# A fused pool and attention layer: three edits to the order of the work in the later projection slots

## The chip, the cores and the metric

The kernel runs on one core of a Trainium2 chip. A core has five engines that run their own instruction queues in order: TensorE (PE, matrix products; its weight loads are listed as PEld), VectorE (DVE), ScalarE (ACT), GpSimd (POOL) and SyncE (SP, which here issues the transfers). The metric is the device time of one execution, in microseconds (us), lower is better. The kernel before takes 346.24 us, the median of three runs (345.97 to 347.31).

## What is computed

One decoder layer over 1024 tokens of width 1024, in float32:

```
h = rmsnorm(x, norm_pre)
pool_u, pool_gate, q, k, v, attn_gate = split(h @ w_in)        # 512, 512, 512, 128, 128, 512 columns
pool  = (mean over the last 2/4/8/16 tokens of pool_u - pool_u) @ pool_w * pool_scale * silu(pool_gate)
attn  = sliding_window_attention(q, k, v, sinks) * silu(attn_gate)
y     = concat(pool, attn) @ w_out
out   = x + rmsnorm(y, norm_post)
```

## The kernel before

Every large product is made of float16 parts. A weight chunk of 1024 rows and 128 columns is bounded (`bound_w`, the sum of absolute values of each row, on ACT), the bound is spread over the partitions by a transpose on PE (`spread`, L82, one buffer `ps_sp`), `scale_w` takes a power of two from it on DVE (L87, L73 to L77, L213), `high_w` writes the high half on ACT (L219) and `low_w` the rest on DVE (L223). `proj` (L283) then makes three products for each of eight steps k: high by high, high by low, low by high; 24 products of 512 columns in all, into one of two accumulators (`ps_acc`).

The program's middle is a loop over slots `s` (L780). A slot is one chunk of columns for one half (512) of the tokens: slots 0 to 9 are k and q, 10 to 17 the pool gate, 18 to 25 `u` (the pool's input), 26 to 33 the attention's gate. The order within a slot is written out by hand, and each engine follows it in order. In the slots that matter here, 20 to 33, it is, in the kernel before:

- `pool_windows` (L482, on DVE): the window sums of the `u` part that landed in the slot before, one to four additions `win` (L489) and a subtraction `res` (L495).
- `low_w` of a chunk whose high half was made in the slot before, then the low parts of the output weights, `low_wo` (L563, on DVE), by a table (L802): one in each of slots 24 and 25, none in 26 and 27, two in each of 28 to 30 as far as their high parts exist, and so on.
- `proj`, with `middle` called ahead of step 4 of 8: there stand the `spread` and scale of the chunk that is due three slots later (in slots 23 to 26) or of a block of 128 tokens of the concatenation (`scale_cat`, in slots 31 to 33), `high_w`, and the pool's product `pool_mm` (L504, `mixed`) of the sums made one slot earlier.
- on ACT then `bound_w` or `bound_cat`, then `split_wo` (L560), the high part of one of the eight chunks of the output weights (slots 23 to 30), and then the slot's landing: `land_u` (L472, `ug`) or the gate's SiLU (`gt`, L529), which empties the accumulator.

After slot 33 comes the output loop (L861): for each block of 128 tokens two groups of 24 products `y`, which walk the output weights' chunks in the order 4, 5, 6, 7, 0, 1, 2, 3.

Of the kernel before, what the change touches and what calls it, by code (L numbers as in the profile page):

```python
# [22 lines left out]
KT = D // P  # L23
# [12 lines left out]
def trunk(ctx: ExitStack, tc, x, w_in, pool_w, pool_scale, attn_sinks, w_out, norm_pre, norm_post, out):  # L36
# [168 lines left out]
    halves = {}  # L205
# [15 lines left out]
    def low_w(ch):  # L221
        w, s = whl[ch], halves.pop(ch)
        nc.vector.scalar_tensor_tensor(  # L223
            w[:, 1], raws.pop(ch), s, w[:, 0], op0=ALU.mult, op1=ALU.subtract
        )
# [54 lines left out]
        split(pv, DOWN, vst[:, 0, tt, :], vst[:, 1, tt, :])  # L280


    def proj(ch, half, middle=None):  # L283
        w = whl[ch]
        acc = ps_acc.tile([P, 512], F32, tag="acc", name="acc")
        for k in range(KT):
            if k == 4 and middle:
                middle()
            for i, (a, b) in enumerate(PASSES):
                nc.tensor.matmul(  # L290
                    acc, w[:, a, k, :], hT[:, b, k, half_of(half)],
                    start=k == 0 and i == 0, stop=k == KT - 1 and i == 2,
                )
        return acc
# [172 lines left out]
    pool_in, pool_out, pool_acc = {}, {}, {}  # L467
# [175 lines left out]
    with tc.manual_schedule(engines={ENG.PE, ENG.Activation, ENG.DVE, ENG.Pool, ENG.SP}):  # L643

        nc.scalar.dma_start(pre, norm_pre[0:1, :])
        load_x(0)
        load_x(1)
        load_w(K)
        load_x(2)
        load_x(3)  # L650
        load_w(V)
        load_w(QS[0])
        load_w(QS[1])
        load_x(4)
        load_x(5)
        accs = {0: ps_acc.tile([P, 512], F32, tag="acc", name="acc")}

        def part(tt):
            products(accs[0][:, block_of(tt)], [
                (whl[K][:, a, k, :], hT[:, b, k, block_of(tt)]) for a, b in PASSES for k in range(KT)  # L660
            ])

        def unit(s):
            ch, half = slots[s]
            accs[s] = proj(ch, half)

        def land_unit(s):
            land_slot(*slots[s], accs.pop(s))

        gains()  # L670
        norm_scan(0)
        norm_scale(0)
        flip(0)
        norm_scan(1)
        norm_scale(1)
        bound_w(K)
        spread_w((K,))
        flip(1)
        norm_scan(2)
        scale_w((K,))  # L680
        norm_scale(2)
        norm_scan(3)
        land_hi(0)
        high_w(K)
        land_lo(0)
        norm_scale(3)
        flip(2)
        low_w(K)
        load_w(QS[2])
        load_x(6)  # L690
        land_hi(1)
        bound_w(V)
        spread_w((V,))
        land_lo(1)
        flip(3)
        scale_w((V,))
        land_hi(2)
        land_lo(2)
        land_hi(3)
        high_w(V)  # L700
        part(0)
        land_lo(3)
        low_w(V)
        load_w(QS[3])
        load_x(7)
        bound_w(QS[0])
        bound_w(QS[1])
        for tt in range(1, 4):
            part(tt)
        spread_w((QS[0], QS[1]))  # L710
        norm_scan(4)
        land_unit(0)
        scale_w((QS[0], QS[1]))
        high_w(QS[0])
        high_w(QS[1])
        norm_scale(4)
        low_w(QS[0])
        low_w(QS[1])
        load_constants()
        v_tile(0)  # L720
        v_tile(1)
        norm_scan(5)
        v_tile(2)
        v_tile(3)
        bound_w(QS[2])
        norm_scale(5)
        unit(1)
        bound_w(QS[3])
        norm_scan(6)
        spread_w((QS[2], QS[3]))  # L730
        flip(4)
        flip(5)
        norm_scan(7)
        norm_scale(6)
        land_hi(4)
        land_hi(5)
        scale_w((QS[2], QS[3]))
        land_lo(4)
        high_w(QS[2])
        high_w(QS[3])  # L740
        unit(2)
        land_lo(5)
        norm_scale(7)
        land_unit(1)
        low_w(QS[2])
        low_w(QS[3])
        flip(6)
        flip(7)
        land_hi(6)
        land_lo(6)  # L750
        unit(3)
        land_hi(7)
        land_lo(7)
        land_unit(2)
        v_tile(4)
        v_tile(5)
        constants()
        unit(4)
        land_unit(3)
        v_tile(6)  # L760
        v_tile(7)
        land_unit(4)
        scale_v()
        scale_qk()


        loads = iter(PGS + US + AGS)

        def load_next():
            ch = next(loads, None)  # L770
            if ch:
                load_w(ch)

        for _ in range(4):
            load_next()

        wo_hi = wo_lo = 0
        state = {"wo": False}
        last = len(slots)
        for s in range(5, last):  # L780
            ch, half = slots[s]
            n, odd = (s - 5) // 2, (s - 5) % 2
            if not odd:
                if 2 <= n <= NB + 1:
                    pv_land(n - 2)
                if 1 <= n <= NB:
                    mask(n - 1)
                if n < NB:
                    score_mm(n)
            elif n < NB:  # L790
                turn(n)
            if 20 <= s < 24:
                gate = cat[:, s - 20, :]
                nc.scalar.activation(gate, gate, AF.Silu)
            gates = list(pool_out)
            for key in list(pool_in):
                pool_windows(*key)

            for c2 in list(halves):
                low_w(c2)  # L800
                load_next()
            for _ in range((1, 1, 1, 0, 0, 2, 2, 2, 2, 2, 2)[s - 23] if s >= 23 else 0):  # L802
                if wo_lo < wo_hi:
                    low_wo(wo_lo)
                    wo_lo += 1


            def middle():
                for key in list(bounds):
                    if key[0] in ("wo", "c"):  # L810
                        spreads[key] = spread(bounds.pop(key))
                        if key[0] == "c":
                            scale_cat(key[1])
                        else:
                            pow2_of(widest(spreads.pop(key)), wop, wos, 14)
                            state["wo"] = True
                    elif first_slot[key] == s + 3:
                        spread_w((key,))
                        scale_w((key,))
                        high_w(key)  # L820
                if not odd and 1 <= n <= NB:
                    divide(n - 1)
                for key in gates:
                    pool_mm(*key)

            acc = proj(ch, half, middle)
            if odd and 1 <= n <= NB:
                pv_mm(n - 1)
            if odd and n < NB:
                turn_low(n)  # L830

            for c2 in order:
                if first_slot[c2] == s + 5:
                    bound_w(c2)

            if 9 <= s < 9 + KT:
                wo_raw["b", s - 9] = load_wo(s - 9)
            if 11 <= s < 11 + KT:
                bound_wo(s - 11)
            if s == 11 + KT:  # L840
                m = bounds["wo", 0] = col("wom")
                nc.vector.tensor_reduce(m, wom, axis=AX.X, op=ALU.max)
            if s >= 30:
                bound_cat(s - 30)
            if s >= 23 and wo_hi < KT:
                split_wo(wo_hi)
                wo_hi += 1
            if not odd and n < NB:
                score_land(n)
            for key in gates:  # L850
                pool_gate(*key)
            land_slot(ch, half, acc)
            if not odd and n < NB:
                exps(n)
            if s == 5 + 2 * NB + 1:
                open_late()
            if 21 <= s < 21 + KT:
                wo_raw["o", s - 21] = load_wo(s - 21)
            if s >= last - 2:
                load_res(s - last + 2)  # L860
        for n in range(NB):  # L861
            if n + 2 < NB:
                load_res(n + 2)
            if n + 4 < NB:
                bound_cat(n + 4)
            if n == NB - 1:
                out_last(n)
                break
            accs = []
            for nh in range(2):  # L870
                accs.append(out_mm(n, nh))
                for key in list(bounds)[:1]:
                    spreads[key] = spread(bounds.pop(key))
                    scale_cat(key[1])
            out_store(n, accs)
# [32 lines left out]
```

## Time and profile before

| | before |
|---|---|
| median of three runs | 346.24 us (345.97 to 347.31) |
| the profiled execution | 346.77 us |
| span of its instructions | 345.1 us, 1.67 us less |
| PE busy | 323.6 us, 94% of the span |
| DVE busy | 199.1 us, 58% |
| ACT busy | 168.9 us, 49% |
| POOL busy | 66.2 us, 19% |

The busy shares are averages over stages that have different limits. A row of the timeline has the start in us from the span's start, the time it took, the engine, line, operation, what is written and read, and in brackets the engine's idle time just before it and what ended that. The times of products overlap: a product that starts 0.216 us after another still shows 0.38 us.

### The profile page before, as it was taken

The numbers are of one execution on the slowest core, as the hardware profiler recorded it, in microseconds if no ns is written. First come the engines' busy times: TensorE is split into PE (matmuls) and PEld (weight loads), VectorE is DVE, ScalarE is ACT, GpSimd is POOL, SyncE is SP. The second block draws the span as 40 slices with busy tenths as digits, with TensorE's granted clock in tenths as the row PEclk, the third lists the DMA queues.
The fourth block names the chain that finished last, engine by engine and source line by source line (L and its number), as shares of the span: only waits on it lengthen the run. The fifth ranks groups of instructions, "written<-read, shape, count | busy, mean of one in ns | idle before, by whom it ended". The sixth has DMA issues, their size and how long they took to land.

```text
span 345.1 us, 5054 instructions
## 1 busy us (share of the span) xinstructions
PE 323.6 (94%) x1913; PEld 166.4 (48%) x1913; DVE 199.1 (58%) x423; ACT 168.9 (49%) x368; POOL 66.2 (19%) x73
## 2 busy tenths in 40 slices
PE   4689999999999999999979998799999999999993
PEld 2588556545444445445434443344444444444442
DVE  4976771537697445796979567793563633410222
ACT  4966831275656685878484443354463433211011
POOL 1100303000132344050423000000000333212330
PEclk9969999999999999999999999999999999999999
DMA  7986240001437367395240892010000241233111
GB/s 280 255 230 159 86 123 0 2 19 44 122 122 208 120 164 179 66 181 126 62 122 0 291 245 76 0 63 0 0 2 0 68 150 59 90 123 122 61 63 61
DMA packets 52090, 35.73 MB, mean 104 GB/s; under 512 B 35041, under 2 KB 45793, under 8 KB 52066
## 3 DMA queue, kind: packets, MB, share of 16 engines
q1 hardware_dynamic: 52064, 35.40, 37.1%
q8 instruction: 15, 0.25, 0.3%
q14 instruction: 9, 0.07, 0.1%
q10 hardware_dynamic: 2, 0.00, 0.0%
HBM read 27.01 MB, written 4.19 MB: 90 GB/s over the span
## 4 chain that ended last, share of the span: by engine, by line
PE 46%; DVE 19%; issue 16%; ACT 9%; POOL 6%; DMA 2%; POOLq 0%; DVEq 0%; SPq 0%; ACTq 0%
PE acc L290 30%; POOL o L639 5%; ACT st L387 4%; PE pv L272 3%; PE y L272 3%; DVE whl L223 3%; DVE st L375 2%; PE tp L250 2%; DVE win L489 2%; PE acc L272 2%; PE sc L358 2%; DVE sc L374 2%; DVE o L636 2%; PE pvo L453 1%; DVE negm L380 1%
## 5 line engine op out<-in xcount | busy, mean ns | idle before, releaser
L290 PE MATMUL acc<-hT,whl 128*128 128x512 f16 x792 | 176.7, 379 | 1.1 <-ACT gt L529 1.1
L290 PEld LDWEIGHTS <-whl 128*128 128x128 f16 x792 | 76.6, 98 | 93.9 <-issue 8.3
L272 PE MATMUL y<-wo,chl 128*128 128x512 f16 (+2 forms) x408 | 83.6, 366 | 0.0
L272 PEld LDWEIGHTS <-chl 128*128 128x128 f16 x408 | 39.0, 98 | 43.5
L219 ACT ACTIVATE whl<-wraw,ws 128x1024 f16<-128x1024 f32 x18 | 20.4, 1148 | 34.6 <-DVE wu L213 22.4
L609 ACT ACTIVATE junk<-y 128x512 bf16<-128x512 f32 (+2 forms) x17 | 9.7, 572 | 54.9 <-PE y L272 54.9
L387 ACT ACTIVATE st<-st,negm 128x129 f32<-128x129 f32 x64 | 24.8, 390 | 12.6 <-DVE negm L380 9.6
L611 DVE SCALAR_TENSOR_TENSOR eps_of<-yss,eps_of 128x1 f32<-128x1 f32 x17 | 3.2, 185 | 45.9 <-ACT junk L609 45.9
L631 POOL TENSOR_TENSOR yf<-eps_of,mhalf 128x1 f32<-128x1 f32 x7 | 3.9, 551 | 119.2 <-DVE eps_of L611 119.2
L223 DVE SCALAR_TENSOR_TENSOR whl<-wraw,ws,whl 128x1024 f16<-128x1024 f32 x18 | 23.7, 1327 | 0.0
L402 DVE SCALAR_TENSOR_TENSOR ph<-st,ph 128x1024 f16<-128x1024 f32 x8 | 9.8, 1226 | 21.6 <-ACT ph L397 21.6
L91 ACT ACTIVATE whl<-wraw 128x1024 bf16<-128x1024 f32 x18 | 18.8, 1049 | 1.5 <-DMA wraw<-in_w_in_dram 1.5
L639 POOL TENSOR_TENSOR o<-o,xr 128x512 f32<-128x512 f32 x14 | 17.5, 1269 | 9.1 <-DVE o L636 9.1
L425 POOL TENSOR_SCALAR_AFFINE_SELECT own<-full 128x2048 f16<-128x2048 f16 x7 | 14.5, 2071 | 22.9 <-DMA full<-ph 22.9
L411 POOL COPY r<-sums 128x512 f32<-128x512 f32 x8 | 4.9, 612 | 67.7 <-DVE sums L409 45.8
L250 PE MATMUL tp<-ident,h 128*128 128x128 f32 x64 | 10.9, 331 | 6.6 <-DVE h L241 3.4
L95 DVE SCALAR_TENSOR_TENSOR chl<-cat,cs,chl 128x1024 f16<-128x1024 f32 x8 | 10.3, 1284 | 10.2 <-ACT chl L94 10.2
L94 ACT ACTIVATE chl<-cat,cs 128x1024 f16<-128x1024 f32 x8 | 9.2, 1148 | 13.7 <-DVE cs L77 13.7
L375 DVE SCALAR_TENSOR_TENSOR st<-sc,qu,bias 128x256 f32<-128x256 f32 x32 | 15.2, 484 | 1.0
L429 POOL TENSOR_SCALAR_AFFINE_SELECT full<-full 128x2048 f16<-128x2048 f16 x7 | 14.4, 2055 | 0.5
L250 PEld LDWEIGHTS tp<-ident,h 128*128 128x128 f32 x64 | 9.1, 172 | 7.9 <-DVE h L241 3.8
L358 PE MATMUL sc<-kT,qT 64*128 64x256 f16 (+1 forms) x192 | 11.6, 263 | 0.6 <-DVE qT L95 0.4
(109 smaller groups left out, 371.9 us busy)
## 6 DMA issues: line engine op xcount, KB each, us to landing
wraw<-in_w_in_dram SPq DMA_DIRECT2D x10, 512.0 KB, 5.1
x<-in_x_dram SPq DMA_DIRECT2D x8, 512.0 KB, 5.4
wraw<-in_w_in_dram SPq DMA_DIRECT2D x16, 256.0 KB, 4.6
woraw<-in_w_out_dram SPq DMA_DIRECT2D x8, 512.0 KB, 5.5
woraw<-in_w_out_dram SPq DMA_DIRECT2D x16, 256.0 KB, 6.8
xr<-in_x_dram SPq DMA_DIRECT2D x8, 512.0 KB, 3.7
out_dram<-o SPq DMA_DIRECT2D x16, 256.0 KB, 2.0
post<-in_norm_post_dram SPq DMA_DIRECT2D x1, 512.0 KB, 4.2
```

The costliest lines, as they stand in the source:

```text
L91: nc.scalar.activation(junk, src, AF.Abs, accum_out=m)
L219: nc.scalar.activation(whl[ch][:, 0], raws[ch], AF.Copy, scale=halves[ch])
L223: nc.vector.scalar_tensor_tensor(w[:, 1], raws.pop(ch), s, w[:, 0], op0=ALU.mult, op1=ALU.subtract)
L250: nc.tensor.transpose(flips[tt][b][:, block_of(i)], h[:, block_of(4 * b + i)], ident)
L272: nc.tensor.matmul(acc, a, b, start=i == 0, stop=i == len(pairs) - 1)
L290: nc.tensor.matmul(acc, w[:, a, k, :], hT[:, b, k, half_of(half)], start=k == 0 and i == 0, stop=k == KT - 1 and i == 2,)
L358: nc.tensor.matmul(banks[kv][:, ci, k0:, :], qT[rows, a, 2 * pr + ci, block_of(n)], kT[rows, b, (n - 1 + k0) * P : (n + 1) * P], start=i = ...
L375: nc.vector.scalar_tensor_tensor(st[:, hs, :P], sc[:, :, 0 if n else 1, :], qu[:, 2 * pr : 2 * pr + 1], (bias if n else bias0)[:, hs, :], ...
L387: nc.scalar.activation(st[:, h, :], st[:, h, :], AF.Exp, bias=negm[:, h : h + 1], accum_out=sums[:, h : h + 1],)
L425: nc.gpsimd.affine_select(o, f, pattern=[[0, 16], [1, P]], compare_op=ALU.is_ge, fill=0.0, base=0, channel_multiplier=-1,)
L429: nc.gpsimd.affine_select(f, f, pattern=[[0, 16], [-1, P]], compare_op=ALU.is_ge, fill=0.0, base=-1, channel_multiplier=1,)
L639: nc.gpsimd.tensor_tensor(o[:, hs], o[:, hs], xr[:, hs], op=ALU.add)
```

## The change

From slot 20 on (`LATE`), the spread and the scale of weights and blocks stand ahead of step 1 of `proj`, where they stood ahead of step 4, and so ahead of the window sums and low parts on DVE, which are now written behind `proj`. The landing stands ahead of `split_wo` on ACT. The low parts of the output weights come one in each slot from 26 to 33, where the table put them in 24 to 31.

```diff
--- before.py
+++ after.py
@@ -280,10 +280,12 @@
         split(pv, DOWN, vst[:, 0, tt, :], vst[:, 1, tt, :])
 
 
-    def proj(ch, half, middle=None):
+    def proj(ch, half, middle=None, early=None):
         w = whl[ch]
         acc = ps_acc.tile([P, 512], F32, tag="acc", name="acc")
         for k in range(KT):
+            if k == 1 and early:
+                early()
             if k == 4 and middle:
                 middle()
             for i, (a, b) in enumerate(PASSES):
@@ -774,6 +776,8 @@
         for _ in range(4):
             load_next()
 
+
+        LATE = 20
         wo_hi = wo_lo = 0
         state = {"wo": False}
         last = len(slots)
@@ -793,19 +797,19 @@
                 gate = cat[:, s - 20, :]
                 nc.scalar.activation(gate, gate, AF.Silu)
             gates = list(pool_out)
-            for key in list(pool_in):
-                pool_windows(*key)
-
-            for c2 in list(halves):
-                low_w(c2)
-                load_next()
-            for _ in range((1, 1, 1, 0, 0, 2, 2, 2, 2, 2, 2)[s - 23] if s >= 23 else 0):
-                if wo_lo < wo_hi:
-                    low_wo(wo_lo)
-                    wo_lo += 1
-
-
-            def middle():
+
+            def sums():
+                for key in list(pool_in):
+                    pool_windows(*key)
+
+
+            def lows():
+                for c2 in list(halves):
+                    low_w(c2)
+                    load_next()
+
+
+            def scales():
                 for key in list(bounds):
                     if key[0] in ("wo", "c"):
                         spreads[key] = spread(bounds.pop(key))
@@ -818,12 +822,29 @@
                         spread_w((key,))
                         scale_w((key,))
                         high_w(key)
+
+            def middle():
+                if s < LATE:
+                    scales()
                 if not odd and 1 <= n <= NB:
                     divide(n - 1)
                 for key in gates:
                     pool_mm(*key)
 
-            acc = proj(ch, half, middle)
+            ready = list(halves)
+            if s < LATE:
+                sums()
+                lows()
+                acc = proj(ch, half, middle)
+            else:
+                acc = proj(ch, half, middle, scales)
+                sums()
+                for c2 in ready:
+                    low_w(c2)
+                    load_next()
+                if s >= 26 and wo_lo < wo_hi:
+                    low_wo(wo_lo)
+                    wo_lo += 1
             if odd and 1 <= n <= NB:
                 pv_mm(n - 1)
             if odd and n < NB:
@@ -842,14 +863,14 @@
                 nc.vector.tensor_reduce(m, wom, axis=AX.X, op=ALU.max)
             if s >= 30:
                 bound_cat(s - 30)
-            if s >= 23 and wo_hi < KT:
-                split_wo(wo_hi)
-                wo_hi += 1
             if not odd and n < NB:
                 score_land(n)
             for key in gates:
                 pool_gate(*key)
             land_slot(ch, half, acc)
+            if s >= 23 and wo_hi < KT:
+                split_wo(wo_hi)
+                wo_hi += 1
             if not odd and n < NB:
                 exps(n)
             if s == 5 + 2 * NB + 1:
```

On DVE, this stood in slot 25 before (`amall` to `wu` is the scale, `win` and `res` are the window sums, `whl` and `wo` the low parts of a chunk and of an output weight, `cat` the pool's gate):

```order
L489 TENSOR_TENSOR win<-ug 128x527 [waits Activation_49]
L489 TENSOR_TENSOR win<-win 128x525 [waits DVE_49]
L489 TENSOR_TENSOR win<-win 128x521 [waits DVE_49]
L495 SCALAR_TENSOR_TENSOR res<-win,ug 128x512 [waits DVE_49]
L223 SCALAR_TENSOR_TENSOR whl<-wraw,ws,whl 128x1024 [waits DMAHW3_49]
L564 SCALAR_TENSOR_TENSOR wo<-woraw,wos,wo 128x1024 [waits DMAHW4_49]
L87 TENSOR_REDUCE amall<-spread 128x1 [waits PE_49]
L73 TENSOR_SCALAR wp<-amall 128x1 [waits DVE_49]
L76 TENSOR_SCALAR wp<-wp 128x1 [waits DVE_49]
L77 RECIPROCAL ws<-wp 128x1 [waits DVE_49]
L213 TENSOR_TENSOR wu<-wp,gsc 128x1
L511 SCALAR_TENSOR_TENSOR cat<-mixed,pscale,cat 128x512 [waits PE_49]
```

and this stands there now:

```order
L87 TENSOR_REDUCE amall<-spread 128x1 [waits PE_49]
L73 TENSOR_SCALAR wp<-amall 128x1 [waits DVE_49]
L76 TENSOR_SCALAR wp<-wp 128x1 [waits DVE_49]
L77 RECIPROCAL ws<-wp 128x1 [waits DVE_49]
L213 TENSOR_TENSOR wu<-wp,gsc 128x1
L491 TENSOR_TENSOR win<-ug 128x527 [waits Activation_49]
L491 TENSOR_TENSOR win<-win 128x525 [waits DVE_49]
L491 TENSOR_TENSOR win<-win 128x521 [waits DVE_49]
L497 SCALAR_TENSOR_TENSOR res<-win,ug 128x512 [waits DVE_49]
L223 SCALAR_TENSOR_TENSOR whl<-wraw,ws,whl 128x1024 [waits DMAHW3_49,DMAHW2_49]
L513 SCALAR_TENSOR_TENSOR cat<-mixed,pscale,cat 128x512 [waits PE_49]
```

The scale went from behind the sums and both low parts to ahead of them, and the low part of the output weight left this slot.

On ACT, slot 24 before (`whl` by L219 is the high half, `whl,as` the bound, `wo` is `split_wo`, `ug` the landing):

```order
L219 ACTIVATE whl<-wraw,ws 128x1024 [waits DVE_49,Activation_49]
L91 ACTIVATE whl,as<-wraw 128x1024 [waits DMAHW7_49,DMAHW0_49]
L561 ACTIVATE wo<-woraw,wos 128x1024 [waits DMAHW4_49]
L474 ACTIVATE ug<-acc,wu 128x512 [waits PE_49,Activation_49]
L476 COPY ug<-tails 128x16
```

and now:

```order
L219 ACTIVATE whl<-wraw,ws 128x1024 [waits DVE_49,Activation_49]
L91 ACTIVATE whl,as<-wraw 128x1024 [waits DMAHW7_49,DMAHW0_49]
L476 ACTIVATE ug<-acc,wu 128x512 [waits PE_49,Activation_49]
L478 COPY ug<-tails 128x16
L563 ACTIVATE wo<-woraw,wos 128x1024 [waits DMAHW4_49]
```

The landing and its tail went ahead of the output weight's high part.

On DVE, slot 33, the last one, before (`amall` to `cs` is the scale of a block, `chl` its low part, `cat<-cat,gt` the gate's product):

```order
L87 TENSOR_REDUCE amall<-spread 128x1 [waits PE_49]
L73 TENSOR_SCALAR cp<-amall 128x1 [waits DVE_49]
L76 TENSOR_SCALAR cp<-cp 128x1 [waits DVE_49]
L77 RECIPROCAL cs<-cp 128x1 [waits DVE_49]
L95 SCALAR_TENSOR_TENSOR chl<-cat,cs,chl 128x1024 [waits Activation_49]
L588 TENSOR_TENSOR e<-cs,wos 128x1
L589 TENSOR_SCALAR eps_of<-e 128x1 [waits DVE_49]
L531 TENSOR_TENSOR cat<-cat,gt 128x512 [waits Activation_49]
```

and now:

```order
L87 TENSOR_REDUCE amall<-spread 128x1 [waits PE_49]
L73 TENSOR_SCALAR cp<-amall 128x1 [waits DVE_49]
L76 TENSOR_SCALAR cp<-cp 128x1 [waits DVE_49]
L77 RECIPROCAL cs<-cp 128x1 [waits DVE_49]
L95 SCALAR_TENSOR_TENSOR chl<-cat,cs,chl 128x1024 [waits Activation_49]
L590 TENSOR_TENSOR e<-cs,wos 128x1
L591 TENSOR_SCALAR eps_of<-e 128x1 [waits DVE_49]
L566 SCALAR_TENSOR_TENSOR wo<-woraw,wos,wo 128x1024 [waits DMAHW6_49,DMAHW5_49]
L533 TENSOR_TENSOR cat<-cat,gt 128x512 [waits Activation_49]
```

The last low part of the output weights came in ahead of the gate's product, where slot 33 had none.

## Rows read from the trace of the kernel before

**Rows 1.** The page, busy time of each engine (share of the span) x instructions
```profile
PE 323.6 (94%) x1913; PEld 166.4 (48%) x1913; DVE 199.1 (58%) x423; ACT 168.9 (49%) x368; POOL 66.2 (19%) x73
```

**Rows 2.** Waits of PE, 165 to 345 us: total, times, longest
```profile
PE rb L440 <- DVE cat L463: 1.8, 1, 1.8
PE spread L82 <- DVE amall L87: 1.5, 1, 1.5
PE acc L290 <- ACT gt L529: 1.1, 1, 1.1
PE mixed L506 <- DVE res L495: 0.8, 1, 0.8
```

**Rows 3.** Timeline of PE, slots 24 to 28, and slot 33
```profile
198.47 1.02 PE L506 MATMUL mixed<-res,pw 128*128 128x512 f32 x2
...
204.62 1.02 PE L506 MATMUL mixed<-res,pw 128*128 128x512 f32 x2
...
212.48 1.02 PE L506 MATMUL mixed<-res,pw 128*128 128x512 f32 x2
213.34 5.34 PE L290 MATMUL acc<-hT,whl 128*128 128x512 f16 x24
219.52 1.12 PE L506 MATMUL mixed<-res,pw 128*128 128x512 f32 x2 [0.83 <-DVE res L495]
220.48 2.75 PE L290 MATMUL acc<-hT,whl 128*128 128x512 f16 x12
224.34 18.29 PE L290 MATMUL acc<-hT,whl 128*128 128x512 f16 x84 [1.11 <-ACT gt L529]
...
253.05 0.27 PE L82 MATMUL spread<-ident,as 128*128 128x128 f32 x1
```

**Rows 4.** Timeline of DVE, slot 25
```profile
206.76 0.71 DVE L489 TENSOR_TENSOR win<-ug 128x527 f32<-128x527 f32 x1 [3.30 <-ACT ug L476]
...
208.98 0.69 DVE L495 SCALAR_TENSOR_TENSOR res<-win,ug 128x512 f32<-128x512 f32 x1
209.59 1.28 DVE L223 SCALAR_TENSOR_TENSOR whl<-wraw,ws,whl 128x1024 f16<-128x1024 f32 x1
210.79 1.28 DVE L564 SCALAR_TENSOR_TENSOR wo<-woraw,wos,wo 128x1024 f16<-128x1024 f32 x1
211.98 0.28 DVE L87 TENSOR_REDUCE amall<-spread 128x1 f32<-128x128 f32 x1
...
212.76 0.14 DVE L213 TENSOR_TENSOR wu<-wp,gsc 128x1 f32<-128x1 f32 x1
```

**Rows 5.** Timeline of ACT, the landings of slots 24 and 25
```profile
205.97 0.67 ACT L474 ACTIVATE ug<-acc,wu 128x512 f32<-128x512 f32 x1
...
212.94 1.15 ACT L219 ACTIVATE whl<-wraw,ws 128x1024 f16<-128x1024 f32 x1 [6.20 <-DVE wu L213]
213.99 1.13 ACT L561 ACTIVATE wo<-woraw,wos 128x1024 f16<-128x1024 f32 x1
215.03 0.67 ACT L474 ACTIVATE ug<-acc,wu 128x512 f32<-128x512 f32 x1
```

**Rows 6.** Timelines of ACT and DVE, slots 32 and 33
```profile
251.03 0.19 ACT L91 ACTIVATION_READ_ACCUMULATOR chl<-cat 128x1 f32 x1
...
254.32 1.15 ACT L94 ACTIVATE chl<-cat,cs 128x1024 f16<-128x1024 f32 x1 [2.53 <-DVE cs L77]
...
253.36 0.29 DVE L87 TENSOR_REDUCE amall<-spread 128x1 f32<-128x128 f32 x1 [0.84 <-PE spread L82]
...
255.50 1.28 DVE L95 SCALAR_TENSOR_TENSOR chl<-cat,cs,chl 128x1024 f16<-128x1024 f32 x1 [1.28 <-ACT chl L94]
...
256.89 0.21 DVE L589 TENSOR_SCALAR eps_of<-e 128x1 f32<-128x1 f32 x1
```

**Rows 7.** Timeline of DVE, around the start of slot 21
```profile
176.54 0.75 DVE L511 SCALAR_TENSOR_TENSOR cat<-mixed,pscale,cat 128x512 f32<-128x512 f32 x1 [1.03 <-ACT cat L794]
177.24 0.67 DVE L463 TENSOR_TENSOR cat<-pvo,cat 128x512 f32<-128x512 f32 x1
```

## The prediction

> **What bounds the kernel now.** I read the page first: PE is busy for 94% of the span, VectorE for 58%, ScalarE for 49% [rows 1]. So the time is the products plus whatever PE waits for, and a faster VectorE is worth nothing unless PE waits for it. Next I asked for PE's waits from 165 us to the end, the part that the change can reach. There are only four: 1.8 us for VectorE's `cat`, 1.5 us in front of a `spread`, 1.1 us for an accumulator, 0.8 us in front of a `mixed` [rows 2]. From slot 28 to the end of the span PE waits for no one.
>
> Then the timeline of PE places them. A slot with a spread and a pool product takes 6.15 us when nothing is late: from `mixed` at 198.47 to `mixed` at 204.62 [rows 3]. One product of 512 columns costs 0.216 us, from the 84 in a row that take 18.29 us, less the 0.16 us by which the last one overhangs [rows 3]. With these two I count what each wait really costs, restart included:
>
> - Slot 26: `mixed` is due at 204.62 + 6.15 = 210.77 and starts at 212.48, **1.71 us late**. The spread ahead of it found the single spread buffer still unread by VectorE (the 1.5 of rows 2).
> - Slot 27: from 213.34, 24 products later, `mixed` is due at 218.52 and starts at 219.52, **1.00 late**, waiting for the window sums [rows 3].
> - Slot 28: from 220.48, 12 products later, the slot is due at 223.07 and starts at 224.34, **1.27 late**, waiting for the accumulator of slot 26, which ScalarE had not emptied [rows 3].
>
> Sum 3.98 us, where the waits alone are 3.4 [rows 2]; the rest is restarts.
>
> The reason stands in VectorE's and ScalarE's timelines. The landing of slot 24 starts at 205.97 on ScalarE [rows 5]. VectorE is idle for 3.30 us until it has that landing, then does the sums (206.76 to 209.67), the low part of a chunk (209.59), the low part of an output weight (210.79), and only then the scale (`amall` 211.98, `wu` ends 212.90) [rows 4]. ScalarE is idle for 6.20 us for that scale, then makes the high half (212.94), the output weight's high part (213.99), and only then the next landing at 215.03 [rows 5]. That is a ring through both engines, one turn per slot: 215.03 - 205.97 = 9.06 us, against 6.15 us of PE work. PE starts ahead, and the ring has used that up by slot 26. Neither engine is full: 6.20 and 3.30 us of each turn are idle. The order makes the ring, not the amount of work.
>
> **The change, part by part.**
>
> *Scales ahead of the sums.* In the changed order `amall` to `wu` stand ahead of the sums and the low parts. The scale of a slot then doesn't need that slot's sums, so the high half, the bound and the landing behind it on ScalarE don't either; the ring now takes two slots for a turn. I lay the slots out without waits: slot 24 starts at 198.47 - 12 x 0.216 - 0.11 (the spread) = 195.77, slot 26 at 208.07, slot 27 at 214.22, slot 28 at 220.26. In slot 26, the fullest, the spread starts three products in, at 208.72; `amall` follows 0.31 later, as from 253.05 to 253.36 [rows 3, 6]; `wu` ends 0.92 after that [rows 4], at 209.95. The sums of slot 26 have four steps where those of rows 4 have three (2.91 us, a fourth adds 0.74): they end at 213.60. The pool product that needs them is due at 216.81. So 3.2 us are to spare where 1.00 was lost. The spread buffer was read a slot earlier, about 5 us ahead of its need. Price of the move on PE: none, since the spread is the same 0.11 us wherever it stands.
>
> *Landings ahead of output weights.* The landing no longer stands behind a high part of 1.13 us [rows 5]. Slot 26 is over at 214.22; with 0.31 us for the crossing and 0.67 for the landing the accumulator is free at 215.2, 5 us before slot 28 wants it.
>
> Together the two remove all three losses. Each edit alone might do for some of them; I don't split the 3.98.
>
> *Low parts from slot 26 on.* They leave slots 24 and 25, 1.28 us each [rows 4], where the ring was. Their new place is one in each slot to the last. What is queued behind them on VectorE is the gate's product of the slot, and behind it the next scale. In slots 31 to 33 one turn on VectorE is: scale to high part 0.96, to the block's low part 1.18, to the end of `eps` 1.60 [rows 6], an output low part 1.20, the gate's product 0.67 (the same size as that at 177.24 [rows 7]), 5.61 in all. The slot is 24 x 0.216 + 0.11 = 5.29. So VectorE loses 0.32 us per slot there. It enters slot 31's scale when slot 30's gate is done, 0.31 + 0.67 + 0.67 = 1.65 us into the slot, thus slot 33's at 2.29, and the last low part ends at 2.29 + 0.96 + 1.18 + 1.60 + 1.28 = 7.31 us into slot 33. The output products want it as the eleventh of the first group, at 5.29 + 10 x 0.216 = 7.45. **Margin 0.14 us.** I take no wait; if I am short it is up to one low part, 1.28 us. Below nothing it can't go, because PE doesn't wait there now.
>
> *Spreads nine products earlier in slots 31 to 33.* There the spread waits for ScalarE's bound of a block. In slot 33 the bound's last step ended at 251.22 [rows 6] and the spread came at 253.05 [rows 3], 1.83 us later. Moved up by 9 x 0.216 = 1.94 us, the spread would wait 0.11 us if the bound kept its place. The bound moves up too: on ScalarE it stands right behind the high part of the block before, whose scale starts 1.65 to 2.29 us into the slot by the reckoning above, where it started 12 x 0.216 + 0.31 = 2.90 us into it. So 0.6 to 1.25 us are won, and 0.5 to 1.1 us of air is left. Cost taken: 0; bounds 0 and 3 x 1.94.
>
> *Transfers.* No weight chunk is left to load after slot 19, so the moved `load_next` issues nothing. The first residual load waits for the buffer that the first low part frees, two slots later than now; its data is wanted only after slot 33. The other queues keep their order.
>
> *The fourth wait* (1.8 us, slot 21) stays. VectorE's `cat` at 177.24 stands behind the pool's gate at 176.54, and that one waited 1.03 us for ScalarE [rows 7], not for the scale or the sums.
>
> **Sum.** The profiled execution took 346.77 us; less 3.98 this is 342.79. The median of the runs is 0.53 lower, 346.24, which gives **342.3 us**. A measurement of this kernel can tell about 0.5%, 1.7 us, so the bound of "faster" is 344.5.
>
> **Rivals.**
>
> *VectorE is held by its own queue.* `amall` now stands ahead of the sums and waits for PE. Before, VectorE stood 0.84 us idle for a spread in slot 33 [rows 6]; the same wait in slots 24 to 26 would now hold the sums. Slot 26 has 0.92 + 3.65 + 1.20 + 1.20 + 0.67 + 0.67 = 8.3 us of VectorE work against 6.15; if these 2.2 us reached PE, the time would be 344.5. For it: nothing else in the slot is as full. Against: 3.2 us to spare, and the landing that the sums need ends 0.31 + 0.67 = 0.98 us into the slot, no earlier than the scale can start (0.65 + 0.31). Chance 0.11. The Trainium skill, page "TensorE: Matmul & The Clock Gate", section "Architectural detail: the array is 16× 32×32, not 1× 128×128", says that ScalarE and VectorE take their instructions strictly first in, first out; by that rule the sums cannot slip past a scale that waits. The 3.30 us of rows 4, idle with the low parts queued behind the sums, agree.
>
> *The early spreads turn into the bound, and it is slower.* Place: PE at step 1 of slots 31, 32 and 33, waiting for a block's bound. Price: up to 1.94 us in each, 5.82 in all, 342.3 + 5.8 = 348.1. It ends slower only if nearly all of this is lost, over 5.7 us; below that it only eats the gain. For it: VectorE's turn of 5.61 exceeds the slot. Against: the excess is 0.32 us a slot, the air 0.5 or more. Chance 0.04.
>
> *The fourth wait goes as well.* The output weights' scale in slot 20 leaves its place between the sums and the attention's low part. Then 1.83 less, 340.4. Against: the chain of rows 7 passes through ScalarE. Chance 0.03.
>
> That the order doesn't change as said is not open: the listing of VectorE's queue shows the scale ahead.
>
> **How the numbers follow.** The forecast has 0.82. The cases of 340.4 and 342.3 are faster, and a little of the first rival, 0.86; the rest of the first rival is within 0.5%, 0.10; the second rival slower, 0.04. The range is 341.0 to 344.4: the lower end takes in part of the fourth wait and the runs' spread of 0.3 below their median; the upper end adds the 1.28 us of the last low part and most of 1 us of the first rival.
>
> **What would show it.** Right: in the changed profile PE's waits of 1.5, 0.8 and 1.1 us are gone, `mixed` follows `mixed` every 6.15 us through slot 26, ScalarE's idle 6.20 us for `wu` shrinks, the first `y` comes some 4 us earlier, and the 1.8 us wait still stands. Wrong: a PE wait for VectorE's `wo` at the first `y`, a PE wait for ScalarE at a spread in slots 31 to 33, or a `mixed` that still waits for `res`.

## The result and the profile after

The changed kernel takes **341.77 us** (median of four runs, 341.63 to 341.83) against 346.22 us before: ratio 0.987, 95% interval 0.9856 to 0.9884. The forecast was 342.3 us, with a range of 341.0 to 344.4. Measured a second time, beside other kernels and with other runs of the kernel before, the two stood at 342.56 and 346.44 us, ratio 0.989 (0.9868 to 0.9911).

| | before | after |
|---|---|---|
| the profiled execution | 346.77 us | 341.63 us |
| its span | 345.1 us | 339.9 us |
| PE's waits from slot 20 to the end | four, 5.3 us | one, 1.8 us |

PE's waits from 160 us to the end, in the changed kernel; the columns are those of [rows 2]:

```profile
PE rb L442 <- DVE cat L465: 1.8, 1, 1.8
```

Of the four rows before, the three of slots 26 to 28 are gone, and the one of slot 21 stands as it was. Busy times are all but those of [rows 1], since no work was removed: PE 322.6 us, VectorE 198.3, ScalarE 169.6.

PE's timeline in the slots of [rows 3]:

```profile
197.44 1.02 PE L508 MATMUL mixed<-res,pw 128*128 128x512 f32 x2
...
203.58 1.02 PE L508 MATMUL mixed<-res,pw 128*128 128x512 f32 x2
...
209.73 1.02 PE L508 MATMUL mixed<-res,pw 128*128 128x512 f32 x2
...
215.77 1.02 PE L508 MATMUL mixed<-res,pw 128*128 128x512 f32 x2
216.63 18.94 PE L292 MATMUL acc<-hT,whl 128*128 128x512 f16 x87
...
240.69 0.27 PE L82 MATMUL spread<-ident,as 128*128 128x128 f32 x1
...
245.98 0.27 PE L82 MATMUL spread<-ident,as 128*128 128x128 f32 x1
...
250.62 5.34 PE L272 MATMUL y<-wo,chl 128*128 128x512 f16 x24
```

`mixed` follows `mixed` every 6.14 or 6.15 us up to slot 26, and slot 27's comes 6.04 us later, as it has no spread. Slot 28 starts 12 products behind 216.63, at 219.22, with no wait. From slot 24's `mixed` to the first `y` the kernel now needs 250.62 - 197.44 = 53.18 us; before it was 57.28 (255.75 - 198.47), so **4.10 us** left this stretch. The row of the first `y` in the kernel before:

```profile
255.75 5.34 PE L272 MATMUL y<-wo,chl 128*128 128x512 f16 x24
```

VectorE's timeline in slot 26, the fullest one, with the scale's start and the sums' start and end, then the scales' starts in slots 31 to 33 and the last low part:

```profile
207.99 0.29 DVE L87 TENSOR_REDUCE amall<-spread 128x1 f32<-128x128 f32 x1 [0.54 <-PE spread L82]
...
208.83 0.70 DVE L491 TENSOR_TENSOR win<-ug 128x527 f32<-128x527 f32 x1
...
211.77 0.69 DVE L497 SCALAR_TENSOR_TENSOR res<-win,ug 128x512 f32<-128x512 f32 x1
...
236.29 0.28 DVE L87 TENSOR_REDUCE amall<-spread 128x1 f32<-128x128 f32 x1
...
241.74 0.28 DVE L87 TENSOR_REDUCE amall<-spread 128x1 f32<-128x128 f32 x1
...
247.19 0.28 DVE L87 TENSOR_REDUCE amall<-spread 128x1 f32<-128x128 f32 x1
...
250.85 1.28 DVE L566 SCALAR_TENSOR_TENSOR wo<-woraw,wos,wo 128x1024 f16<-128x1024 f32 x1
```

The scale comes first (207.99), then the sums (from 208.83). They end at 212.46 and are read at 215.77. ScalarE's timeline, from the landing of slot 24 to that of slot 26, and the last steps of two bounds of blocks:

```profile
201.15 0.69 ACT L476 ACTIVATE ug<-acc,wu 128x512 f32<-128x512 f32 x1 [2.31 <-PE acc L292]
...
207.23 0.69 ACT L476 ACTIVATE ug<-acc,wu 128x512 f32<-128x512 f32 x1 [3.22 <-PE acc L292]
...
207.91 1.15 ACT L563 ACTIVATE wo<-woraw,wos 128x1024 f16<-128x1024 f32 x1
208.96 1.14 ACT L219 ACTIVATE whl<-wraw,ws 128x1024 f16<-128x1024 f32 x1
213.44 0.69 ACT L531 ACTIVATE gt<-acc,wu 128x512 f32<-128x512 f32 x1 [3.34 <-PE acc L292]
...
239.24 0.19 ACT L91 ACTIVATION_READ_ACCUMULATOR chl<-cat 128x1 f32 x1
...
244.70 0.19 ACT L91 ACTIVATION_READ_ACCUMULATOR chl<-cat 128x1 f32 x1
```

The high half starts right behind the output weight's high part (207.91, 208.96) with no idle time, where ScalarE was idle for 6.20 us [rows 5], and the landings are 201.15, 207.23, 213.44: one per 6.1 to 6.2 us. That is the pace of PE, and the rows' brackets name PE as what each landing waited for, where in [rows 5] the landings had no idle time ahead of them.

**Where the rest of the difference is from.** The spans differ by 5.2 us, the stretch by 4.10 (57.28 - 53.18). The `mixed` of slot 20, ahead of which PE's order differs only in the place of that slot's spread, came 1.03 us earlier in the changed kernel's execution already (167.46 against 168.49). A difference that shows ahead of it is the clock. In the view of stretches the columns are busy us and count of each engine, the granted TensorE clock, DMA share and GB/s. Before:

```profile
15.00:20.00 5.00, 3.02 (x17) 2.45 (x18) 4.90 (x11) 2.45 (x5) 0.00 (x0) 0.69 0.91 283
20.00:25.00 5.00, 5.00 (x58) 4.94 (x57) 3.52 (x6) 4.73 (x9) 0.00 (x0) 0.62 0.73 189
```

and after:

```profile
15.00:20.00 5.00, 3.66 (x17) 3.26 (x18) 4.90 (x11) 2.64 (x5) 0.00 (x0) 1.00 0.94 283
20.00:25.00 5.00, 5.00 (x77) 4.94 (x76) 3.50 (x6) 4.73 (x9) 0.00 (x0) 1.00 0.61 177
```

In the one execution the clock stood at the lower of its two levels (1.2 GHz instead of 2.4) for part of 15 to 25 us, in the other it didn't. The changed kernel's own runs show both: with a mean clock of 0.993 to 0.999 they took 341.63 to 342.16 us, with 0.985 342.46 to 343.14. The clock need not be all of it: in the trace of *scales alone* below, at a clock of 1.00 in both stretches, the same `mixed` stands at 167.93. So the experiments below are read by the stretch from slot 24's `mixed` to the first `y` first, and then by the time.

### The profile page after: what moved, and what is told of

The parts are those of the page before. It is cut to its first block, busy times and chain, and to the rows that moved or that the text cites. A ratio compares the mean times of both kernels' runs of the same rounds, so it can differ in the third digit from the quotient of the medians.

```text
span 339.9 us, 5053 instructions
## 1 busy us (share of the span) xinstructions
PE 322.6 (95%) x1913; PEld 166.8 (49%) x1913; DVE 198.3 (58%) x423; ACT 169.6 (50%) x368; POOL 66.1 (19%) x73
## 4 chain that ended last, share of the span: by engine, by line
PE 60%; issue 14%; DVE 10%; POOL 8%; ACT 5%; DMA 2%; POOLq 0%; DVEq 0%; ACTq 0%
PE acc L292 41%; POOL o L641 5%; PE pv L272 3%; PE y L272 3%; ACT st L389 3%; PE tp L250 2%; PE sc L360 2%; PE pvo L455 2%; PE mixed L508 2%; PE acc L272 2%; DVE o L638 2%; DMA full<-ph 1%; DVE st L377 1%; PE gain L176 1%; POOL yf L633 1%
## 5 line engine op out<-in xcount | busy, mean ns | idle before, releaser
L219 ACT ACTIVATE whl<-wraw,ws 128x1024 f16<-128x1024 f32 x18 | 20.4, 1145 | 15.9 <-DVE ws L77 12.3
L250 PE MATMUL tp<-ident,h 128*128 128x128 f32 x64 | 11.7, 350 | 5.9 <-DVE h L241 3.4
L531 ACT ACTIVATE gt<-acc,wu 128x512 f32<-128x512 f32 x8 | 5.5, 687 | 18.9 <-PE acc L292 15.4
L250 PEld LDWEIGHTS tp<-ident,h 128*128 128x128 f32 x64 | 9.9, 182 | 7.3 <-DVE h L241 3.8
```

The lines of the kernel that those rows point to most:

```text
L219: nc.scalar.activation(whl[ch][:, 0], raws[ch], AF.Copy, scale=halves[ch])
L250: nc.tensor.transpose(flips[tt][b][:, block_of(i)], h[:, block_of(4 * b + i)], ident)
```

## The experiments

The theory: PE's three losses came from a ring through VectorE and ScalarE (landing, sums, low parts, scale, high half, high part, next landing) that took 9.06 us per slot against PE's 6.15. The rivals were that each edit carries a share, that the sums have to be behind the scale, and that hidden slack or something else that is late next decides what the tail and the fourth wait are worth. Each ratio is to the runs of the kernel before that were made beside it; the stretch in the last column is that of one trace each.

| kernel | median us | ratio to before (95%) | slot 24's `mixed` to first `y`, us |
|---|---|---|---|
| before | 346.22 to 346.59 | | 57.28 |
| the change | 341.77; again 342.56 | 0.987 (0.9856 to 0.9884); 0.989 (0.9868 to 0.9911) | 53.18; 53.19 |
| scales alone | 342.15 | 0.9887 (0.9863 to 0.991) | 53.18 |
| landings alone | 343.18 | 0.9901 (0.9879 to 0.9922) | 53.54 |
| output low parts alone | 346.09 | 0.9987 (0.9975 to 0.9999) | 57.77 |
| the change, low parts from slot 27 | 342.86 | 0.9897 (0.9878 to 0.9915) | 53.19 |
| all low parts behind the scale | 342.49 | 0.9881 (0.9854 to 0.9908) | 53.20 |
| the change, gate product moved | 341.68 | 0.9861 (0.9839 to 0.9883) | 53.19 |
| the same, and pool product moved | 340.82 | 0.9836 (0.9812 to 0.986) | 53.18 |

**Scales alone.** The changed kernel with the other two edits undone:

```diff
@@ -845,3 +845,4 @@
-                if s >= 26 and wo_lo < wo_hi:
-                    low_wo(wo_lo)
-                    wo_lo += 1
+                for _ in range((1, 1, 1, 0, 0, 2, 2, 2, 2, 2, 2)[s - 23] if s >= 23 else 0):
+                    if wo_lo < wo_hi:
+                        low_wo(wo_lo)
+                        wo_lo += 1
@@ -865,0 +867,3 @@
+            if s >= 23 and wo_hi < KT:
+                split_wo(wo_hi)
+                wo_hi += 1
@@ -871,3 +874,0 @@
-            if s >= 23 and wo_hi < KT:
-                split_wo(wo_hi)
-                wo_hi += 1
```

> Only the scales go ahead of the sums; the landings stand behind split_wo and the low parts follow the old table. Theory (the ring through VectorE and ScalarE was made by the scale's place alone): PE's waits of 1.5, 0.8 and 1.1 us are gone without the other two edits, the time is that of the changed kernel, 341.8 us within 0.4. Rival (the other edits were needed to shorten the ring, each carries a share): a wait of PE for an accumulator or for res stays in slots 26 to 28, 0.5 to 2 us, and the time is 342.3 to 343.8.

The theory held. PE's timeline, slot 24's `mixed` and the first `y`:

```profile
197.91 1.02 PE L508 MATMUL mixed<-res,pw 128*128 128x512 f32 x2
...
251.09 5.34 PE L272 MATMUL y<-wo,chl 128*128 128x512 f16 x24
```

PE has no wait in these slots, and the stretch takes 53.18 us, to the hundredth as with all three edits. This edit alone is enough. It is not one step, though: it puts the spread earlier, the scale ahead of the sums and the low parts behind the scale.

**Landings alone.** The kernel before, with one edit:

```diff
@@ -845,3 +844,0 @@
-            if s >= 23 and wo_hi < KT:
-                split_wo(wo_hi)
-                wo_hi += 1
@@ -852,0 +850,3 @@
+            if s >= 23 and wo_hi < KT:
+                split_wo(wo_hi)
+                wo_hi += 1
```

> Only the landings go ahead of split_wo. Theory: the ring stays, one turn per slot, but without the 1.13 us of the output weight it takes 9.06 - 1.13 = 7.9 us against PE's 6.15; as PE's lead is used up only by slot 26, laying the slots out gives waits of 0.6 us in all instead of 4, so about 342.4. Rival (an edit that does not break the ring gives only its own length, 1.13 us or little more): 345.0.

The same two rows of PE's timeline:

```profile
199.10 1.02 PE L506 MATMUL mixed<-res,pw 128*128 128x512 f32 x2
...
252.64 5.34 PE L272 MATMUL y<-wo,chl 128*128 128x512 f16 x24
```

The stretch takes 53.54 us, 0.36 us more than with the change; 0.6 was forecast. The median, 343.18, is 0.8 us above the forecast 342.4: the two runs with a mean clock of 0.998 and 0.999 took 342.45 and 342.71 us, the two with 0.985 and 0.989 took 343.66 and 343.67. The rival, that 1.13 us out of the ring give 1.13 us, is out by far: 3.74 of 4.10 us went. The ring is still there, only shorter, as ScalarE's landings of slots 24 and 25 show:

```profile
204.94 0.67 ACT L474 ACTIVATE ug<-acc,wu 128x512 f32<-128x512 f32 x1
...
212.96 0.67 ACT L474 ACTIVATE ug<-acc,wu 128x512 f32<-128x512 f32 x1
```

A turn takes 8.02 us, where 9.06 - 1.13 = 7.93 was to be expected. As I read it, the ring's excess over PE's slot counts once in every slot and is paid only when PE's lead is used up; a shorter ring pays later, and the slots with sums are over by then.

**Output low parts alone.** The kernel before, with another table:

```diff
@@ -802 +802 @@
-            for _ in range((1, 1, 1, 0, 0, 2, 2, 2, 2, 2, 2)[s - 23] if s >= 23 else 0):
+            for _ in range(1 if s >= 26 else 0):
```

> Only the low parts of the output weights come one in each slot from 26 on, ahead of proj as before. Theory: two times 1.2 us leave the ring in slots 24 and 25, one comes into slot 26, so the wait at the spread of slot 26 goes, the one for the accumulator in slot 28 grows to 2 us or more; 1.2 us are won, about 345.0. Rival (amount of work ahead of the scale is what counts): the gain is 2.4 us or more, 343.8 or less.

As forecast the wait at the spread went and that for the accumulator grew, to 2.30 us. But the stretch became longer, 57.77 us against 57.28. PE's timeline:

```profile
197.43 1.02 PE L506 MATMUL mixed<-res,pw 128*128 128x512 f32 x2
...
216.09 1.12 PE L506 MATMUL mixed<-res,pw 128*128 128x512 f32 x2 [0.15 <-DVE res L495]
...
222.10 19.98 PE L290 MATMUL acc<-hT,whl 128*128 128x512 f16 x84 [2.30 <-ACT gt L529]
...
255.20 5.34 PE L272 MATMUL y<-wo,chl 128*128 128x512 f16 x24
```

The 84 products from 222.10 take 19.98 us, where they took 18.29 before [rows 3]. The view of stretches shows the clock (columns as above, the clock is the third number from the end):

```profile
222.10:224.00 1.90, 1.90 (x7) 0.70 (x6) 1.90 (x3) 1.90 (x3) 0.00 (x0) 0.68 0.04 9
224.00:226.00 2.00, 2.00 (x6) 0.73 (x5) 2.00 (x3) 0.71 (x1) 0.00 (x0) 0.50 0.00 0
226.00:228.00 2.00, 2.00 (x10) 0.91 (x9) 1.63 (x2) 0.00 (x0) 0.00 (x0) 0.95 0.82 260
```

Behind the 2.30 us in which PE stood, the clock fell to its lower level (0.68, 0.50 and 0.95 of full in these pieces) and cost 1.69 us. Without that the stretch would be 56.08, 1.20 us less than before, which is the forecast. The rival's 2.4 us is out. So the mechanism was as forecast, and the time was not: 345.0 forecast, 346.09 measured, since in the profiled execution at least the clock took back more than was won. Its mean clock was 0.992, and the five runs with 0.992 or 0.993 took 346.19 to 346.95 us. The four with 0.986 or 0.987 took 345.81 to 345.99, about 1 us less than the runs of the kernel before with 0.985 to 0.990 (346.70 to 347.31). These look like the forecast gain without the late fall of the clock, but no trace of them was kept.

**The change with the low parts one slot later still.**

```diff
@@ -845 +845 @@
-                if s >= 26 and wo_lo < wo_hi:
+                for _ in range(2 if s == 33 else 1 if s >= 27 else 0):
```

> The changed kernel with the low parts one slot later still: one in each slot from 27, two in slot 33. In the changed kernel's trace the last low part ended 0.65 us ahead of the product that reads it. Theory (that margin was all there was, and nothing else in the tail is late): the last low part comes 1.2 us later, PE waits 0.5 to 0.7 us for it in the first output group, 342.4 us. Rival (there is hidden slack, or the wait is passed on and multiplied in the output loop): no change, 341.8, or over 343.

PE's timeline of the first output group and the spread behind it:

```profile
251.50 2.35 PE L272 MATMUL y<-wo,chl 128*128 128x512 f16 x10
254.24 3.18 PE L272 MATMUL y<-wo,chl 128*128 128x512 f16 x14 [0.39 <-DVE wo L566]
257.26 0.27 PE L82 MATMUL spread<-ident,as 128*128 128x128 f32 x1
```

PE waits 0.39 us for the last low part, as the tenth product of the group is done; the group's spread comes 5.76 us behind its start where the changed kernel has 5.19 (250.62 to 255.81), so 0.57 us is lost in all. The forecast was a wait of 0.5 to 0.7. The median, 342.86 us, is 0.5 above the forecast 342.4; two of the four runs had a mean clock of 0.989. The place of the low parts in the change is one slot short of costing something.

**All low parts behind the scale, and nothing else.** The sums stay ahead of the scale, the spread at step 4:

```diff
@@ -799,7 +799,5 @@
-            for c2 in list(halves):
-                low_w(c2)
-                load_next()
-            for _ in range((1, 1, 1, 0, 0, 2, 2, 2, 2, 2, 2)[s - 23] if s >= 23 else 0):
-                if wo_lo < wo_hi:
-                    low_wo(wo_lo)
-                    wo_lo += 1
+            ready = list(halves)
+            if s < 20:
+                for c2 in ready:
+                    low_w(c2)
+                    load_next()
@@ -826,0 +825,8 @@
+            if s >= 20:
+                for c2 in ready:
+                    low_w(c2)
+                    load_next()
+            for _ in range((1, 1, 1, 0, 0, 2, 2, 2, 2, 2, 2)[s - 23] if s >= 23 else 0):
+                if wo_lo < wo_hi:
+                    low_wo(wo_lo)
+                    wo_lo += 1
```

> The kernel before, with only the low parts of chunks and output weights moved behind the scale on VectorE from slot 20 on; the sums stay ahead of the scale, the spread ahead of step 4, the landings behind split_wo. Theory (what counts is all work between a landing and the next scale): without the two times 1.2 us the ring takes about 7 us a turn with the sums, PE's lead lasts past slot 28, and PE has no waits of 0.3 us or more in slots 24 to 28: as the changed kernel, within 0.5 us. Rival (the sums must be behind the scale, or the ring stays): at least one wait of 0.5 to 1.5 us in slots 26 to 28.

PE's timeline, the two rows that bound the stretch:

```profile
198.67 1.02 PE L506 MATMUL mixed<-res,pw 128*128 128x512 f32 x2
...
251.87 5.34 PE L272 MATMUL y<-wo,chl 128*128 128x512 f16 x24
```

PE has no wait in it, and it takes 53.20 us; the median, 342.49, is that of the changed kernel beside it, 342.56. So the sums need not be behind the scale. ScalarE's landings of slots 24 and 25:

```profile
203.79 0.67 ACT L474 ACTIVATE ug<-acc,wu 128x512 f32<-128x512 f32 x1
...
210.46 0.67 ACT L474 ACTIVATE ug<-acc,wu 128x512 f32<-128x512 f32 x1
```

A turn takes 6.67 us, and 9.06 less the two low parts of 1.20 is 6.66. It is still longer than PE's 6.15, so the ring isn't broken here either; PE's lead lasts. Taking about 2.4 us out of the way between a landing and the next scale does as well as the change, which is what the theory says and the rival denies.

**The fourth wait.** The changed kernel, with the pool's gate product of slot 20 moved behind slot 21's attention product on VectorE:

```diff
@@ -781,0 +782 @@
+        held = []
@@ -789,0 +791,2 @@
+                while held:
+                    pool_gate(*held.pop(0))
@@ -868,2 +871,5 @@
-            for key in gates:
-                pool_gate(*key)
+            if s == 20:
+                held += gates
+            else:
+                for key in gates:
+                    pool_gate(*key)
```

> The changed kernel with the pool's gate product of slot 20 moved behind the attention product (cat<-pvo,cat) of slot 21 on VectorE, so that this one no longer stands behind ScalarE's SiLU. Theory (the wait of 1.8 us in slot 21 is only queue order on VectorE): it shrinks to 0.3 us or less, but PE then comes 1.6 us earlier to the mixed of slot 22, whose sums end late because a res took 2.37 and a small addition 1.85 us there while GpSimd masked; VectorE gets to them only 0.6 us earlier, so a new wait of about 1 us stands at that mixed and only 0.6 us is won over the changed kernel. Rival (nothing is late next): 1.6 us is won.

PE's timeline in slots 21 and 22:

```profile
172.66 2.76 PE L292 MATMUL acc<-hT,whl 128*128 128x512 f16 x12
175.54 0.66 PE L442 MATMUL rb<-ident,r 128*128 128x128 f32 x4
...
183.26 1.12 PE L508 MATMUL mixed<-res,pw 128*128 128x512 f32 x2 [1.02 <-DVE res L503]
```

`rb` is due at 172.66 + 12 x 0.216 = 175.25 and comes 0.29 us later (it waited 1.84), and a new wait of 1.02 us stands at slot 22's `mixed`. From slot 20's `mixed` (167.70) to slot 24's (197.18) it takes 29.48 us, against 29.98 in the changed kernel (167.46 to 197.44): 0.5 us won, 0.6 forecast. The medians, 341.68 and 342.56 for the changed kernel beside it, are 0.88 us apart, which their intervals don't separate. VectorE's timeline shows why the sums were late:

```profile
177.15 1.44 DVE L491 TENSOR_TENSOR win<-win 128x525 f32<-128x525 f32 x2
178.63 2.49 DVE L497 SCALAR_TENSOR_TENSOR res<-win,ug 128x512 f32<-128x512 f32 x1
181.15 1.85 DVE L502 TENSOR_TENSOR win<-win,invc 128x7 f32<-128x7 f32 x1
```

A `res` of 2.49 us, where slot 26's takes 0.69, and a product of 7 columns that takes 1.85 us. GpSimd's timeline has its two masks over the same time:

```profile
178.57 2.01 POOL L427 TENSOR_SCALAR_AFFINE_SELECT own<-full 128x2048 f16<-128x2048 f16 x1 [3.08 <-DMA full<-ph]
180.65 2.34 POOL L431 TENSOR_SCALAR_AFFINE_SELECT full<-full 128x2048 f16<-128x2048 f16 x1
```

The product ends with the second mask (181.15 + 1.85 = 183.00, 180.65 + 2.34 = 182.99), and `res` 0.54 us behind the first (181.12, 180.58), as if VectorE could do little until the mask was over. That they hold each other up was not tried by itself. The Trainium skill, page "SBUF — State Buffer", section "Who interferes with whom", says that a VectorE instruction with two inputs in SBUF contends with a GpSimd instruction that reads SBUF; these rows agree.

**The same, with slot 22's pool product behind its 24 products.**

```diff
@@ -834,2 +834,3 @@
-                for key in gates:
-                    pool_mm(*key)
+                if s != 22:
+                    for key in gates:
+                        pool_mm(*key)
@@ -850,0 +852,3 @@
+            if s == 22:
+                for key in gates:
+                    pool_mm(*key)
```

> As the kernel with the moved gate product, and the pool product of slot 22 stands behind all 24 products of its slot. Theory: the new wait at that mixed is gone too, since PE comes to it 2.6 us later in its slot, and 1.5 us is won over the changed kernel, about 340.3. Rival: the wait goes on to the attention's products (pvo) or the next accumulator, and the gain stays at 0.6 us.

PE's timeline from slot 20's `mixed` to slot 24's:

```profile
168.94 1.02 PE L508 MATMUL mixed<-res,pw 128*128 128x512 f32 x2
...
178.15 7.93 PE L292 MATMUL acc<-hT,whl 128*128 128x512 f16 x36
185.92 1.02 PE L508 MATMUL mixed<-res,pw 128*128 128x512 f32 x2
...
197.15 1.02 PE L508 MATMUL mixed<-res,pw 128*128 128x512 f32 x2
```

No wait is listed from slot 21 on: 36 products in a row, then `mixed`. From slot 20's `mixed` to slot 24's it takes 197.15 - 168.94 = 28.21 us, 1.77 us less than the change. At 340.82 us, 0.9836 of before (0.9812 to 0.986), it is the fastest of all, 1.74 us below the changed kernel measured beside it (342.56); 1.5 us and 340.3 were forecast.

**The changed kernel again**, unedited:

> The changed kernel again, on the chip of these runs, for comparison: 341.8 us within 0.5 by both theories; the granted clock between 15 and 25 us from the start may be at either of its two levels, which moves the time by up to 1 us.

342.56 us is 0.26 us above the band that was given. Three of its four runs had a mean clock of 0.985, and the profiled one of these shows a clock of 0.65 from 15 to 20 us and 0.67 from 20 to 25. Its stretch, 53.19 us, is that of the first profile.

## Why the prediction was right

- *The sum, 3.98 us.* The stretch lost 4.10. The difference is in slot 27, where the `mixed` that had waited also held PE 0.10 us longer (219.52 to 220.48, against 0.86 us undisturbed); my due times had taken that 0.96 as given. Counting late starts instead of the waits' 3.4 us was right: each wait cost about 0.2 us more than it shows. It is hardly a restart, as the prediction calls it: 0.16 us of each is the overhang of the product before the wait. The row counts idle time from that product's end, and the next one was due 0.16 us ahead of it.
- *The time.* 341.77 against 342.3. Of the missing 0.5 us, 0.12 are the above and the rest is not the change's, as far as the traces tell: the profiled execution before had the low clock early on, and its median stands for a mix of both. The second measurement gave a gain of 3.88 us, the first 4.45. In the second, the runs with a mean clock of 0.985 to 0.989 can be set side by side: 346.83 to 346.91 before, 342.46 to 343.14 changed, medians 4.20 us apart. So what the first measurement shows beyond some 4.1 us is most likely the luck of that mix.
- *The ring.* Shown by three edits that shorten or break it (scales ahead, landings ahead, low parts behind), each of which alone gives 3.7 to 4.1 us; the first of them contains the third. I had left the 3.98 undivided; it can't be divided, since each gives nearly all of it. That the ring now takes two slots for a turn, as the prediction has it, is one way to win them: a ring of one slot gives nearly or fully as much if it is short enough (8.02 and 6.67 us a turn instead of 9.06). And the edit to the output weights' low parts was not needed for them; by itself it won 1.20 us of the stretch and lost 1.69 to the clock.
- *Spare time in slot 26.* Forecast 3.2 us for the sums, measured 3.31 (212.46 to 215.77); forecast 5 us for the accumulator, measured 5.09 (214.13 to 219.22).
- *The last low part.* I gave it 0.14 us of margin, it had 0.65: it ended at 252.13, its product was due at 250.62 + 10 x 0.216 = 252.78. VectorE's turn is 5.45 us (236.29 to 241.74 to 247.19) where I had 5.61, the gate's product and the end of `eps` overlapping with what follows; the first scale came 1.53 us into its slot, not 1.65. Right in sign, a little too dark. One slot later it cost 0.57 us.
- *Early spreads.* Forecast 0.5 to 1.1 us of air; the bounds ended at 239.43 and 244.89, the spreads came at 240.69 and 245.98: 1.26 and 1.09 us, the first a little more than forecast.
- *VectorE held by its own queue.* In slot 26 VectorE stood 0.54 us idle for the spread, ahead of the scale and with the sums behind it (the landing ended just then, at 207.92), and the work ran over into slot 27 without reaching PE. The strict order that the Trainium skill states (page "TensorE: Matmul & The Clock Gate", section "Architectural detail: the array is 16× 32×32, not 1× 128×128") is not contradicted by these 0.54 us; it had no price here.
- *The fourth wait.* It stayed, as argued, and the move of the gate product showed the reason: queue order on VectorE behind ScalarE's SiLU. That removing it would give 1.83 us, the size I used for the rival of 340.4, was too simple: only 0.5 us was won, and a wait of 1.02 us stood at the next `mixed`.

## What to carry to other kernels

When PE waits although two other engines are both idle for long pieces of every turn, follow one result around: if it passes through both engines within one slot, the sum of the pieces is the pace, and one reordering that lets the ring span two slots, or takes enough out of it, can do; here each of three did. Don't add up the gains of several such edits. Before counting a removed wait as won, look up what the engine would reach next and when that is ready.

## What the runs showed of the hardware

- In *output low parts alone* a PE wait of 2.30 us was followed by a granted clock of 0.50 to 0.68 and cost another 1.69 us. Waits of 1.50, 0.83 and 1.11 us in the kernel before had left the clock at 1.00 throughout these slots. That is one trace; where the border lies was not tried.
- Executions of the same code differ ahead of slot 20, where the clock between 15 and 25 us from the start differs: slot 20's `mixed` came at 167.46 us in one trace of the changed kernel (clock 1.00 in both stretches) and at 168.29 in the other (0.65 and 0.67).
- VectorE's `res` of 512 columns took 2.37 to 2.49 us instead of 0.69, and a product of 7 columns 1.85, while GpSimd's masks were running. In the changed kernel a `wu` product of one column took 1.24 us instead of 0.14; it ended at 95.06, and a mask that had started at 93.05 ended at 95.05.
